# The first two column pairs of layer 2's feed-forward as eight plain products by token halves

## The chip, the cores and the metric

The kernel runs on one core of a Trainium2 chip. The metric is device time in microseconds (us) of one execution. Before the change the median of three runs is 1791.24 us (1790.11 to 1793.18). The profiled execution took 1794.53 us, of which its span is 1792.7 us.

## The reference

Two layers of a backbone over 512 latent tokens and 256 context tokens, width 1024, feed-forward width 2816, all in float32. The change is in the feed-forward of layer 2, which only the latent tokens pass:

```python
def _swiglu(h, w_in, w_out):
    g, u = jnp.split(h @ w_in, 2, axis=-1)
    return (jax.nn.silu(g) * u) @ w_out
...
    x = x + g2 * _swiglu(_rmsnorm(x, norm_w[layer, 1]) * (1.0 + sc2) + sh2, ffn_w_in[layer], ffn_w_out[layer])
```

## The kernel before

**Tiling.** Activations are held feature-major: 8 blocks of 128 features by 512 latent tokens. A float32 product is made of three passes in the format fp32r: an operand is split into a high and a low part (`h`, `lo`), and high·high, high·low and low·high are summed in PSUM. ScalarE (ACT) casts the high part, VectorE (DVE) subtracts it to get the low one. So one product over 4 feature blocks and 256 tokens is 12 matmuls of 128x256.

**Seven products instead of eight.** For each of the 22 blocks of 128 columns of the input projection (a *pair*: the block `g` and its partner `u`) the two matrices, split into upper and lower feature rows (r = 0, 1), and the tokens, split into the halves LA and LB, form a 2x2 by 2x2 block product. It is computed with seven products of 12 matmuls instead of eight. They need sums on the activation side (the *forms* `t2`, `t3`, `n1`, `n4` beside the plain `b11`, `b21` of LA and `b12`, `b22` of LB) and sums on the weight side (`z`, `y`, made per pair on DVE in tiles `ws`). Of the seven, only the two with `b11` and `b21` can start with LA alone; the forms of the other five need LB.

**What comes before.** The output projection of attention (`pf`, from `oh`, `ol`) runs first over LA, then over LB. After each half DVE adds it to the stream `xt`, ACT squares it, GpSimd (POOL) adds the squares into `nacc`; TensorE (PE) sums over partitions (`nsum`), DVE adds epsilon (`v`), POOL takes the power -1/2 (`rs`), PE broadcasts it (`nbc`), and `norm_seven` makes the normed and modulated rows (tile `bb`: one DVE and one ACT instruction per feature block) and the forms (tile `hT`). With LA ready, `op_ffn_seven` computes `c11` (products `b11`, `b21`, bank `pg`) of pairs 0 and 1, then waits for LB; `rest` computes the other five products of a pair in banks `pu`. After every four pairs the output projection of four pairs (`outproj`, bank `pf`, from the activations `fu`) follows.

**Order of the work.** The program is recorded by generators ("streams") that a small planner (`Flow.run`) interleaves by estimated times; what is recorded is then in a fixed order on each engine. Each engine takes its instructions strictly in that order, so an instruction that waits holds up all behind it on the same engine. Weights come through `Weights.ask` on SP's DMA queue into three buffers `wr` of 512 KB; a buffer is asked for again when the instructions that split it have been recorded, and the DMA starts when they have run. `Weights.seven` splits a pair: `xh`, `xl` for `g` and for the lower half of `u`, `wh`, `wl` for the sums `z` and `y`.

In the trace nearly all instructions have one line, that of the helper which records them (L107), so tiles tell them apart.

Of the kernel before, what the change touches and what calls it, by code (L numbers as in the profile page):

```python
# [8 lines left out]
F32 = mybir.dt.float32  # L9
# [134 lines left out]
def kernel(ctx, tc, x, c, cx, c_ctx, ada_w, ada_b, norm_w, ffn_w_in, ffn_w_out, ab_w_in,  # L144
# [45 lines left out]
    def t3(name, dt=F32, n=512, bufs=None):  # L190
        return tmp.tile([P, n], dt, tag=name, name=nm(name), bufs=bufs)
# [289 lines left out]
    class Weights:  # L481
# [8 lines left out]
        def plan(self, specs):  # L490

            for sp in specs:
                i = len(self.todo)
                if sp[0] == "seven":
                    self.todo += sp[1:]
                    self.jobs.append((i, i + 1))
                else:
                    self.todo.append(sp)
                    self.jobs.append((i,))
# [34 lines left out]
        def seven(self, i, job):  # L534


            yield lambda: self.asked > job[1] and "pool" in F1
            yield spend((self.n_x, 1))
            flow.cur.t = max(self.at[j] for j in job)
            yield  # L540
            g, u = (self.raw.pop(j) for j in job)
            parts = {}

            def split(name, tiles, src):
                h, lo = tiles
                act.copy(h, src)
                dve.tensor_tensor(lo, src, f(h), ALU.subtract)
                parts[name] = h, lo

            def whl():  # L550
                return tuple(wp.tile([P, KT, P], F32R, tag=t, name=nm(t), bufs=3) for t in ("wh", "wl"))

            def sums():
                return F1["pool"].tile([P, KT, P], F32, tag="ws", name=nm("ws"), bufs=3)

            x = [F1["pool"].tile([P, 12, P], F32R, tag=t, name=nm(t), bufs=2) for t in ("xh", "xl")]
            split("g", [t[:, 0:8] for t in x], g)
            self.units[i] = parts
            yield
            z = sums()  # L560
            y = sums()
            dve.tensor_tensor(y[:, 0:4], g[:, 0:4], u[:, 0:4], ALU.add)
            dve.tensor_tensor(y[:, 4:8], u[:, 0:4], u[:, 4:8], ALU.add)
            yield
            dve.tensor_tensor(z[:, 0:4], y[:, 4:8], g[:, 0:4], ALU.add)
# [1267 lines left out]

    FORMS = ("b11", "b21", "t2", "t3", "n1", "n4", "b22")
    hT, b_ = [], {}

    def form(lo, name, q):

        i = 14 * lo + 2 * FORMS.index(name) + q
        while len(hT) <= i // 3:
            hT.append(big([P, 3, 2, 256], F32R, "hT"))
        return hT[i // 3][:, i % 3]

    def norm_seven(part):
# [8 lines left out]
        def rows(r, q):  # L1855

            name = ("b11", "b21") if first else ("b12", "b22")
            t = b_.get(name[r])
            if t is None:
                if first:  # L1860
                    t = F1["pool"].tile([P, 4, 256], F32, tag="bb", name=nm("bb"), bufs=2)
                else:
                    t = big([P, 6, 256], F32, "bb")
                b_[name[r]] = t
            for k in (2 * q, 2 * q + 1):
                kk = 4 * r + k
                dve.scalar_tensor_tensor(t[:, k], xk(xt, kk, a, b), amod[1][:, 1, kk, 0:1], bcs[:, 0:256],
                                         ALU.mult, ALU.mult)
                act.activation(t[:, k], t[:, k], AF.Identity, bias=mod[1][:, 24 + kk, 0:1])
            return t[:, 2 * q:2 * q + 2]  # L1870

        def two(name, q, src):
            h, lo = form(0, name, q), form(1, name, q)
            act.copy(h, src)
            return lambda: dve.tensor_tensor(lo, src, f(h), ALU.subtract)

        if first:
# [7 lines left out]
            late()  # L1885
            ready["g1done"].add(a)
            return
        late = []
        pair = lambda: t3("hfull").rearrange("p (k n) -> p k n", k=2)
        n1, t2 = [], []  # L1890
        sums = big([P, 3, 2, 256], F32, "bb")
        for q in range(2):
            b12, b22 = rows(0, q), rows(1, q)
            n1.append(sums[:, q])
            t2.append(sums[:, 2] if q else b_["b12"][:, 4:6])
            dve.tensor_tensor(n1[q], b_["b11"][:, 2 * q:2 * q + 2], b12, ALU.subtract)
            dve.tensor_tensor(t2[q], b22, n1[q], ALU.add)
            two("t2", q, t2[q])()
        for q in range(2):
            b12, b22 = (b_[n][:, 2 * q:2 * q + 2] for n in ("b12", "b22"))  # L1900
            t = pair()
            dve.tensor_tensor(t, b12, b22, ALU.subtract)
            two("t3", q, t)()
        for q in range(2):
            two("n1", q, n1[q])()
        for q in range(2):
            t = pair()
            dve.tensor_tensor(t, b_["b21"][:, 2 * q:2 * q + 2], t2[q], ALU.subtract)
            two("n4", q, t)()
        for q in range(2):  # L1910
            two("b22", q, b_["b22"][:, 2 * q:2 * q + 2])()
        ready["g1done"].add(a)

    def norm_then(part):
        def run():
# [7 lines left out]
    def op_ffn_seven(last):  # L1923
# [30 lines left out]
        def rest(fi, c11_later):  # L1954
            u, bank_a, m1 = there[fi][:3]
            pu = psum2("pu")
            bank_b, bank_d = pu[:, 0:256], pu[:, 512:768]
            yield lambda: "z" in u and LB[0] in ready["g1done"]
# [40 lines left out]
        def place(fi):  # L1999
# [6 lines left out]
                res.append(pieces.pop(0))  # L2006
            acts[fi] = res

        def inproj(fi):
            def gen():  # L2010
                place(fi)
                if fi == 0:
                    yield from c11(0)
                    c11_end(0)
                    flow.cur.t = 0.0
                    yield
                    yield from c11(1)
                    c11_end(1)
                    flow.cur.t = 0.0
                    yield  # L2020
                elif fi > 1:
                    yield from c11(fi)
                    flow.cur.t = 0.0
                    yield
                yield from rest(fi, fi > 1)
            c0 = P * fi
            op(gen, [("seven",) + tuple(wfeat(ffn_w_in[1, :, c:c + P]) for c in (c0, DFF + c0))])

        def outproj(fs):
            nk = len(fs)  # L2030
# [29 lines left out]
            else:  # L2060
                op(lambda: gen((LAT,)), specs)

        for fi in range(NF):
            inproj(fi)
            if fi % 4 == 1 and 4 < fi < NF - 4:
                outproj(list(range(fi - 5, fi - 1)))
        outproj(list(range(NF - 6, NF)))

    def store(k, part):
# [90 lines left out]
```

## Time and profile before

| | |
|---|---|
| median of the runs | 1791.24 us |
| profiled execution | 1794.53 us, span 1792.7 us |
| PE busy | 1728.4 us, 96% of the span, 11898 instructions |
| DVE busy | 1153.3 us, 64% |
| ACT busy | 688.7 us, 38% |
| POOL busy | 270.3 us, 15% |
| granted TensorE clock, mean | 0.978 of full speed |

The stretch that the change touches runs from about 1380 us of the span (end of attention's output projection) to about 1480 us (the first pairs); layer 2's feed-forward then goes on to the end. The page's second part shows the span in 40 slices of 45 us each; this stretch is shorter than one slice, so it is read from views of a few microseconds, below.

### The profile page before, as it was taken

The page shows a single profiled execution, that of the slowest core. Times are in us where ns is not written, and L with a number is a line of the kernel's source. Part 1 is how long each engine was busy: PE and PEld are TensorE (multiplying, and loading weights), DVE is VectorE, ACT ScalarE, POOL GpSimd, SP SyncE. Part 2 cuts the span into 40 slices and gives each one's busy share as a digit, 9 for nine tenths or more (in the row PEclk, how much of TensorE's full clock was granted, in tenths as well). Part 3 has the DMA queues.
Part 4 walks back from the last instruction along what each step waited for, and adds up shares of the span by engine and source line. Part 5 has one row for each costly group of instructions (what it writes and reads, how often), then busy time and mean ns, then how long its engine had stood idle before and what let it go on. Part 6 is the DMA issues. An engine that isn't in the chain of part 4 may idle for free.

```text
span 1792.7 us, 29501 instructions
## 1 busy us (share of the span) xinstructions
PE 1728.4 (96%) x11898; PEld 1532.6 (85%) x11898; DVE 1153.3 (64%) x2084; ACT 688.7 (38%) x1348; POOL 270.3 (15%) x265
## 2 busy tenths in 40 slices
PE   7899999999999999999999999898999899999998
PEld 5789899999878888888888888897667788999998
DVE  5855365756597376564544335778886887787785
ACT  4522334433425221212121124545775554443443
POOL 4202120211123000000000003335554300000000
PEclk8999899999999999999999999898999889999999
DMA  9511111111573254353542215221003523233335
GB/s 343 193 51 48 28 45 38 34 36 54 194 241 113 81 177 141 118 165 117 157 147 62 60 52 159 73 71 48 2 1 100 149 58 113 89 117 96 102 87 153
DMA packets 224557, 184.36 MB, mean 103 GB/s; under 512 B 7532, under 2 KB 206628, under 8 KB 224420
## 3 DMA queue, kind: packets, MB, share of 16 engines
q1 hardware_dynamic: 222468, 178.20, 32.6%
q10 hardware_dynamic: 1952, 4.27, 0.7%
q8 instruction: 94, 1.54, 0.4%
q14 instruction: 43, 0.35, 0.1%
HBM read 175.10 MB, written 7.34 MB: 102 GB/s over the span
## 4 chain that ended last, share of the span: by engine, by line
PE 82%; DVE 8%; DMA 3%; ACT 3%; issue 2%; POOL 1%; SPq 0%; DVEq 0%; POOLq 0%; ACTq 0%
PE pf L107 27%; PE pu L107 17%; PE pg L107 13%; PE pt L107 10%; PE sc L107 3%; PE ao L107 2%; DMA wr<-in_ffn_w_in_dram 2%; PE mo L107 2%; PE atr L107 2%; DVE wl L107 1%; PE ro L107 1%; DVE acc L107 1%; PE kv L107 1%; PE me L107 1%; PE ada L107 1%
## 5 line engine op out<-in xcount | busy, mean ns | idle before, releaser
L107 ACT CAST wh<-wr 128x1024 fp32r<-128x1024 f32 (+1 forms) x184 | 186.0, 1011 | 341.3 <-PE pf L107 171.4
L107 DVE TENSOR_TENSOR wl<-wr,wh 128x1024 fp32r<-128x1024 f32 (+1 forms) x184 | 222.6, 1210 | 105.7 <-ACT wh L107 104.6
L107 DVE SCALAR_TENSOR_TENSOR xt<-pf,mod,xt 128x512 f32<-128x512 f32 (+1 forms) x160 | 97.9, 615 | 90.2 <-PE pf L107 89.6
L107 POOL TENSOR_TENSOR nacc<-nacc,sq 128x256 f32<-128x256 f32 (+1 forms) x42 | 54.9, 1308 | 631.7 <-ACT sq L107 628.5
L107 PE MATMUL pu<-hT,wh 128*128 128x256 f32 x704 | 129.0, 284 | 1.8 <-ACT hT L107 1.8
L107 DVE TENSOR_TENSOR hfull<-pu,sq 128x512 f32<-128x512 f32 (+1 forms) x44 | 24.5, 558 | 149.8 <-PE pu L107 149.5
L107 PE MATMUL pf<-fh,wh 128*128 128x256 f32 (+1 forms) x352 | 119.3, 340 | 0.8 <-ACT wh L107 0.8
L107 PE MATMUL pf<-fl,wh 128*128 128x256 f32 (+1 forms) x352 | 118.5, 337 | 0.0
L107 PE MATMUL pf<-fh,wl 128*128 128x256 f32 (+1 forms) x352 | 118.0, 338 | 0.5 <-DVE wl L107 0.5
L107 PE MATMUL pf<-fu,wh 128*128 128x512 f32 (+1 forms) x448 | 116.7, 349 | 1.4 <-ACT fu L107 0.4
L107 DVE SCALAR_TENSOR_TENSOR acc<-aw,cmod,acc 128x1024 f32<-128x1024 f32 x90 | 115.0, 1300 | 0.0
L107 PEld LDWEIGHTS pu<-hT,wh 128*128 128x128 f32 x704 | 108.9, 191 | 3.0 <-ACT hT L107 2.4
L107 PE MATMUL pu<-hT,wl 128*128 128x256 f32 x352 | 97.9, 283 | 0.1
L107 PEld LDWEIGHTS pf<-fu,wh 128*128 128x128 f32 x448 | 77.2, 188 | 12.8 <-ACT fu L107 0.6
L107 PE MATMUL pt<-wh,hh 128*128 128x256 f32 x288 | 84.2, 294 | 3.4 <-ACT hh L107 2.2
L107 PE MATMUL pt<-wl,hh 128*128 128x256 f32 x288 | 83.6, 292 | 0.3 <-DVE wl L107 0.3
L107 PE MATMUL pg<-g0h,wh 128*128 128x512 f32 (+1 forms) x220 | 82.1, 373 | 1.5 <-ACT sq L107 1.5
L107 POOL TENSOR_TENSOR aE<-aE,ast 128x512 f32<-128x512 f32 (+1 forms) x64 | 72.9, 1153 | 66.9 <-DVE ast L107 51.6
L107 PE MATMUL pg<-g0l,wh 128*128 128x512 f32 (+1 forms) x220 | 82.3, 374 | 0.0
L107 PE MATMUL pt<-wh,hl 128*128 128x256 f32 x288 | 82.2, 288 | 0.0
L107 PE MATMUL pu<-g0l,wh 128*128 128x512 f32 (+1 forms) x220 | 82.0, 373 | 0.0
L107 PE MATMUL pu<-g0h,wh 128*128 128x512 f32 (+1 forms) x220 | 81.9, 372 | 0.0
(379 smaller groups left out, 5166.1 us busy)
## 6 DMA issues: line engine op xcount, KB each, us to landing
wr<-in_ffn_w_in_dram SPq DMA_DIRECT2D x88, 512.0 KB, 3.9
aw<-in_ada_w_dram SPq DMA_DIRECT2D x84, 512.0 KB, 5.0
wr<-in_ab_w_in_dram SPq DMA_DIRECT2D x32, 512.0 KB, 4.3
wr<-in_ffn_w_out_dram SPq DMA_DIRECT2D x32, 512.0 KB, 5.2
wr<-in_ffn_w_out_dram SPq DMA_DIRECT2D x32, 384.0 KB, 3.6
wr<-in_ab_w_out_dram SPq DMA_DIRECT2D x16, 512.0 KB
wr<-in_attn_w_out_dram SPq DMA_DIRECT2D x16, 512.0 KB, 4.2
aw<-in_ada_w_dram SPq DMA_DIRECT2D x8, 768.0 KB
```

What stands on the lines that cost most here:

```text
L107: r = fn(*a, **k)
```

## The change

Pairs 0 and 1 are computed with plain products, LA first: for each token half four products per pair (`g` and `u`, upper and lower rows), accumulated in one bank `pg` of 512 columns (left half `g`, right half `u`), then silu, product and split by halves of 256 tokens. Their weights are split as they are (`g` in `xh`, `xl`; all of `u` in `wh`, `wl`), without the sums `z` and `y`. LB's plain rows `b12`, `b22` are made and split first, then the forms, in place of the rows they come from, where before some had tiles of their own. The seven products start with pair 2. The output projection of four pairs follows after pairs 4, 8, 12 and 16 instead of 5, 9, 13 and 17.

```diff
@@ class Weights, seven()
+            if job[2] == "eight":
+                yield spend((self.n_p, 1))
+                split("u", whl(), u)
+                self.freed += 2
+                self.ask()
+                return
             z = sums()
...
-    FORMS = ("b11", "b21", "t2", "t3", "n1", "n4", "b22")
+    FORMS = ("b11", "b21", "b22", "t2", "t3", "n1", "n4", "b12")
...
@@ norm_seven(), part LB
+        for q in range(2):
+            for r in range(2):
+                two(("b12", "b22")[r], q, rows(r, q))()
+        ready["g1done"].add(a)
+        four = [[b_[n][:, 2 * q:2 * q + 2] for n in ("b11", "b21", "b12", "b22")] for q in range(2)]
+        t2 = [b_[n][:, 4:6] for n in ("b12", "b22")]
+        for q, (b11, b21, b12, b22) in enumerate(four):
+            dve.tensor_tensor(b11, b11, b12, ALU.subtract)
+            dve.tensor_tensor(t2[q], b22, b11, ALU.add)
+            two("t2", q, t2[q])()
+        for q, (b11, b21, b12, b22) in enumerate(four):
+            dve.tensor_tensor(b12, b12, b22, ALU.subtract)
+            two("t3", q, b12)()
+        for q, (b11, b21, b12, b22) in enumerate(four):
+            two("n1", q, b11)()
+        for q, (b11, b21, b12, b22) in enumerate(four):
+            dve.tensor_tensor(b21, b21, t2[q], ALU.subtract)
+            two("n4", q, b21)()
+        ready["g1done"].add("forms")
...
@@ op_ffn_seven()
+        PLAIN = 2
+        def plain():
+            us = {}
+            for part, names in ((LA, ("b11", "b21")), (LB, ("b12", "b22"))):
+                c = slice(part[0] - NCX, part[1] - NCX)
+                for fi in range(PLAIN):
+                    if part is LA:
+                        place(fi)
+                        us[fi], = yield from W.take(1)
+                        yield lambda: "u" in us[fi]
+                    yield lambda: part[0] in ready["g1done"]
+                    ps = wide_bank("pg")
+                    for i, t in enumerate("gu"):
+                        for r, name in enumerate(names):
+                            product(ps[:, 256 * i:256 * i + 256], us[fi][t], 4 * r, name, start=r == 0)
+                    if part is LB:
+                        W.give(1)
+                        W.n_x.n += 1
+                    th, tl = acts[fi]
+                    sg, cc = t3("sq")[:, 0:256], t3("hfull")[:, 0:256]
+                    act.activation(sg, ps[:, 0:256], AF.Silu)
+                    dve.tensor_tensor(cc, ps[:, 256:512], sg, ALU.mult)
+                    act.copy(th[:, c], cc)
+                    dve.tensor_tensor(tl[:, c], cc, f(th[:, c]), ALU.subtract)
+                    flow.cur.t = 0.0
+                    yield
...
-        for fi in range(NF):
+        op(plain, [("eight",) + columns(fi) for fi in range(PLAIN)])
+        for fi in range(PLAIN, NF):
             inproj(fi)
-            if fi % 4 == 1 and 4 < fi < NF - 4:
-                outproj(list(range(fi - 5, fi - 1)))
+            if fi % 4 == 0 and 0 < fi < NF - 4:
+                outproj(list(range(fi - 4, fi)))
         outproj(list(range(NF - 6, NF)))
```

On PE, at the end of attention's output projection, the order before was this (`pf` is that projection, `pg` the first product of pair 0; numbers belong to buffers):

```order
L107 MATMUL pf_2166_13929<-ol_2000_12969,wh_2158_13874 128x256
L107 MATMUL pf_2166_13929<-oh_1999_12968,wl_2159_13876 128x256
L107 MATMUL nsum_2172_13970<-cst_74,nacc_94 128x1 x2
L107 MATMUL pg_2174_13976<-hT_2134_13713,xh_2163_13909 128x256
L107 MATMUL pg_2174_13976<-hT_2138_13717,xh_2163_13909 128x256
L107 MATMUL pg_2174_13976<-hT_2134_13713,xl_2164_13910 128x256
```

After the change the same `nsum` and `nbc` stand here on PE (`pg_2171` is pair 0 over LA, `pg_2192` pair 1 over LA):

```order
L107 MATMUL pg_2171_13969<-hT_2135_13720,wh_2164_13939 128x256
L107 MATMUL nsum_2169_13963<-cst_74,nacc_94 128x1 x2
L107 MATMUL pg_2171_13969<-hT_2137_13728,wh_2164_13939 128x256
L107 MATMUL pg_2171_13969<-hT_2135_13720,wl_2165_13940 128x256
L107 MATMUL pg_2171_13969<-hT_2135_13720,wh_2164_13939 128x256
L107 MATMUL pg_2171_13969<-hT_2137_13728,wh_2164_13939 128x256
L107 MATMUL pg_2171_13969<-hT_2135_13720,wl_2165_13940 128x256
L107 MATMUL nbc_2176_14028<-cst_74,rs6_93 128x128 x2
L107 MATMUL pg_2192_14098<-hT_2134_13713,xh_2174_14024 128x256 x2
```

Before, `nsum` stood directly behind the last `pf`, with 12 matmuls between it and `nbc`. Now 43 of the 48 matmuls of pair 0 over LA stand ahead of `nsum`, and only five between it and `nbc`.

On DVE, the step `v` (written `v6`) between `nsum` and `nbc` stood before among sums of pair 1 and pair 2 (`ws`, from the loads `wr`), in this order:

```order
L107 TENSOR_TENSOR wl_2178_14006<-ws_2167_13942,wh_2177_14005 128x1024
L107 TENSOR_SCALAR v6_92<-nsum_2172_13970 128x2
L107 TENSOR_TENSOR wl_2192_14068<-ws_2168_13943,wh_2191_14067 128x1024
L107 TENSOR_TENSOR ws_2195_14075<-ws_2196_14076,wr_2160_13878 128x512
L107 TENSOR_TENSOR ws_2216_14218<-wr_2171_13968,wr_2200_14112 128x512
```

Now it stands here (`wr_2167` and `wr_2190` are the two loads of pair 2, `wr_2166` is `u` of pair 1, `hfull` the first activation product of pair 0):

```order
L107 TENSOR_TENSOR wl_2189_14091<-wr_2166_13943,wh_2188_14090 128x1024
L107 TENSOR_TENSOR ws_2207_14297<-wr_2167_13945,wr_2190_14094 128x512
L107 TENSOR_TENSOR ws_2207_14297<-wr_2190_14094 128x512
L107 TENSOR_TENSOR ws_2206_14296<-ws_2207_14297,wr_2167_13945 128x512
L107 TENSOR_SCALAR v6_92<-nsum_2169_13963 128x2
L107 TENSOR_TENSOR ws_2206_14296<-ws_2206_14296,wr_2167_13945 128x512
L107 TENSOR_TENSOR hfull_2173_14019<-pg_2171_13969,sq_2172_14018 128x256
L107 SCALAR_TENSOR_TENSOR bb_2177_14031<-xt_2084_13370,amod1_176,nbc_2176_14028 128x256 x2
```

Three sums of pair 2 now stand ahead of `v`, the first of which reads both loads of pair 2; before, the first sum over both loads of pair 2 stood behind `v`.

## Rows read from the trace of the kernel before

**Rows 1.** Page, part 4: shares of the chain that ended last, by engine.

```profile
PE 82%; DVE 8%; DMA 3%; ACT 3%; issue 2%; POOL 1%; SPq 0%; DVEq 0%; POOLq 0%; ACTq 0%
```

**Rows 2.** Busy time by stretch: us, each engine with instructions, clock, DMA share, GB/s.

```profile
1380.00:1400.00 20.00, 20.00 (x172) 20.00 (x171) 11.97 (x15) 9.24 (x15) 9.07 (x7) 1.00 0.65 187
...
1417.60:1421.50 3.90, 0.19 (x2) 0.00 (x0) 3.27 (x6) 1.12 (x4) 2.38 (x2) 1.00 0.47 134
1421.50:1445.30 23.80, 17.36 (x72) 15.89 (x73) 20.50 (x35) 13.92 (x26) 1.62 (x1) 0.50 0.23 67
...
1450.00:1750.00 300.00, 299.15 (x2149) 281.08 (x2150) 237.72 (x355) 124.80 (x181) 0.00 (x0) 1.00 0.34 100
```

**Rows 3.** PE in order of time: start, us, instruction [idle before <-releaser].

```profile
1421.52 1.01 PE L107 MATMUL nsum<-cst,nacc 128*128 128x1 f32 x4 [3.73 <-POOL nacc L107]
...
1426.30 1.22 PE L107 MATMUL nbc<-cst,rs 128*128 128x128 f32 x4 [1.00 <-POOL rs L107]
1427.18 0.77 PE L107 MATMUL pg<-hT,xh 128*128 128x256 f32 x2
...
1449.99 0.47 PE L107 MATMUL pu<-hT,xh 128*128 128x256 f32 x2 [0.61 <-DVE u L107]
```

**Rows 4.** PE's groups from 1417.6 to 1449.9, first and last of four.

```profile
L107 PE MATMUL pg<-hT,xh 128*128 128x256 f32 x32 | 10.7, 435 | 3.6 <-ACT sq L107 3.0 <-ACT m L107 0.6
...
L107 PE MATMUL pu<-hT,wl 128*128 128x256 f32 x16 | 5.0, 318 | 0.0
```

**Rows 5.** PE in order of time, at half and at full clock.

```profile
1427.96 0.63 PE L107 MATMUL pg<-hT,xh 128*128 128x256 f32 x2
...
1429.24 0.63 PE L107 MATMUL pg<-hT,xh 128*128 128x256 f32 x2
...
1460.20 0.28 PE L107 MATMUL pu<-hT,wl 128*128 128x256 f32 x1
...
1462.33 0.40 PE L107 MATMUL pu<-hT,wh 128*128 128x256 f32 x2
```

**Rows 6.** Page, part 6: DMA issues, with size and median us to landing.

```profile
wr<-in_ffn_w_in_dram SPq DMA_DIRECT2D x88, 512.0 KB, 3.9
```

**Rows 7.** ACT in order of time, the load of pair 1's g.

```profile
1416.79 1.05 ACT L107 CAST xh<-wr 128x1024 fp32r<-128x1024 f32 x1 [1.93 <-DMA wr<-in_ffn_w_in_dram]
```

**Rows 8.** DVE in order of time, from the first loads to pair 2's sums.

```profile
1413.30 0.47 DVE L107 SCALAR_TENSOR_TENSOR xt<-pf,mod,xt 128x256 f32<-128x256 f32 x1
...
1421.45 0.69 DVE L107 TENSOR_TENSOR ws<-wr,wr 128x512 f32<-128x512 f32 x1 [0.62 <-DMA wr<-in_ffn_w_in_dram]
...
1424.40 0.15 DVE L107 TENSOR_SCALAR v<-nsum 128x2 f32<-128x2 f32 x1
...
1427.92 0.69 DVE L107 TENSOR_TENSOR ws<-wr,wr 128x512 f32<-128x512 f32 x1 [1.64 <-DMA wr<-in_ffn_w_in_dram]
```

**Rows 9.** POOL in order of time, the power after each half's sum.

```profile
1398.64 0.71 POOL L107 TENSOR_TENSOR rs<-v,mhalf 128x2 f32<-128x2 f32 x1 [2.38 <-DVE v L107]
...
1424.63 1.62 POOL L107 TENSOR_TENSOR rs<-v,mhalf 128x2 f32<-128x2 f32 x1 [3.17 <-DVE v L107]
```

**Rows 10.** DVE in order of time, rows and forms of LB, and a later load.

```profile
1402.43 3.22 DVE L107 SCALAR_TENSOR_TENSOR bb<-xt,amod,nbc 128x256 f32<-128x256 f32 x8 [0.62 <-POOL nacc L107]
...
1432.87 1.22 DVE L107 TENSOR_TENSOR wl<-ws,wh 128x1024 fp32r<-128x1024 f32 x1
1434.00 0.69 DVE L107 TENSOR_TENSOR bb<-bb,bb 128x512 f32<-128x512 f32 x1
...
1447.20 0.76 DVE L107 TENSOR_TENSOR u<-pu,m 128x256 f32<-128x256 f32 x2
...
1470.28 0.69 DVE L107 TENSOR_TENSOR ws<-wr,wr 128x512 f32<-128x512 f32 x1 [2.74 <-DMA wr<-in_ffn_w_in_dram]
```

**Rows 11.** Busy time by stretch, around an idle time of PE in attention.

```profile
1230.20:1233.10 2.90, 0.13 (x3) 0.09 (x2) 2.90 (x6) 2.51 (x4) 0.00 (x0) 1.00 0.05 14
1233.80:1244.00 10.20, 8.77 (x40) 7.32 (x38) 9.03 (x23) 5.43 (x15) 4.80 (x3) 0.50 0.28 83
```

More of the change, by code (lines that the diff above doesn't have):

```diff
@@ L493, in plan @@
                 i = len(self.todo)
-                if sp[0] == "seven":
+                if sp[0] in ("seven", "eight"):
                     self.todo += sp[1:]
-                    self.jobs.append((i, i + 1))
+                    self.jobs.append((i, i + 1, sp[0]))
                 else:
@@ L538, in seven @@
             yield spend((self.n_x, 1))
-            flow.cur.t = max(self.at[j] for j in job)
+            flow.cur.t = max(self.at[j] for j in job[:2])
             yield
-            g, u = (self.raw.pop(j) for j in job)
+            g, u = (self.raw.pop(j) for j in job[:2])
             parts = {}
@@ L1832 @@
     LA, LB = (NCX, NCX + 256, 0), (NCX + 256, NT, 0)
-    FORMS = ("b11", "b21", "t2", "t3", "n1", "n4", "b22")
+    FORMS = ("b11", "b21", "b22", "t2", "t3", "n1", "n4", "b12")
     hT, b_ = [], {}
     def form(lo, name, q):
-        i = 14 * lo + 2 * FORMS.index(name) + q
+        i = 4 * FORMS.index(name) + 2 * lo + q
         while len(hT) <= i // 3:
@@ L1887, in norm_seven @@
             return
[L1888 to L1891, printed above, removed]
         for q in range(2):
[L1893 to L1897, printed above, removed]
-            two("t2", q, t2[q])()
[L1899 to L1912, printed above, removed]
+            for r in range(2):
[6 more added lines that the diff above has]
+            dve.tensor_tensor(t2[q], b22, b11, ALU.add)
+            two("t2", q, t2[q])()
+        for q, (b11, b21, b12, b22) in enumerate(four):
[7 more added lines that the diff above has]
+        ready["g1done"].add("forms")
     def norm_then(part):
@@ L1957, in rest @@
             bank_b, bank_d = pu[:, 0:256], pu[:, 512:768]
-            yield lambda: "z" in u and LB[0] in ready["g1done"]
+            yield lambda: "z" in u and "forms" in ready["g1done"]
             product(bank_b, u["z"], 0, "t2")
@@ L2007, in place, with columns @@
             acts[fi] = res
+        def columns(fi):
+            return tuple(wfeat(ffn_w_in[1, :, c:c + P]) for c in (P * fi, DFF + P * fi))
+        PLAIN = 2
[24 more added lines that the diff above has]
+                    yield
         def inproj(fi):
@@ L2011, in gen @@
                 place(fi)
-                if fi == 0:
-                    yield from c11(0)
-                    c11_end(0)
+                if fi == PLAIN:
+                    yield from c11(fi)
+                    c11_end(fi)
                     flow.cur.t = 0.0
                     yield
-                    yield from c11(1)
-                    c11_end(1)
+                    yield from c11(fi + 1)
+                    c11_end(fi + 1)
                     flow.cur.t = 0.0
                     yield
-                elif fi > 1:
+                elif fi > PLAIN + 1:
                     yield from c11(fi)
@@ L2024, in gen @@
                     yield
-                yield from rest(fi, fi > 1)
-            c0 = P * fi
-            op(gen, [("seven",) + tuple(wfeat(ffn_w_in[1, :, c:c + P]) for c in (c0, DFF + c0))])
+                yield from rest(fi, fi > PLAIN + 1)
+            op(gen, [("seven",) + columns(fi)])
         def outproj(fs):
```

## The prediction

> **What bounds the kernel now.** I read the chain that ended last first: PE holds 82% of it [rows 1], so a change pays where PE idles or runs slowly. Busy time by stretch shows where that is. From 1450 to 1750 us PE is busy 299.15 of 300 us at full clock; from 1417.60 to 1421.50 it does next to nothing, and from 1421.50 to 1445.30 it is busy 17.36 of 23.80 us at a granted clock of 0.50, the lower of its two levels, 1.2 GHz [rows 2]. PE in order of time names the waits: 3.73 us for POOL's sum of squares of LB (so PE had ended at 1417.79), then 1.00 for the power, and several more up to 1449.99, after which it runs through [rows 3]. That is the price of norming LB: with LA alone PE had only the 48 matmuls of `c11` of pairs 0 and 1 to do.
>
> The stretch from 1417.79 to 1449.99 is 32.2 us. It holds 96 matmuls of the feed-forward: four groups, the first of 32, the last of 16, and two of the same sizes between [rows 4]. At full clock 18 matmuls take 1462.33 - 1460.20 = 2.13 us, 0.118 each; at half clock six take 1429.24 - 1427.96 = 1.28 us, 0.213 each [rows 5]. So 96 x 0.118 = 11.3 us is work, and **20.9 us are lost** (with `nsum` and `nbc` counted as lost). The change can win at most that.
>
> **The change part by part.**
>
> *Work added.* Two pairs with eight products instead of seven: 2 x 12 = 24 matmuls x 0.118 = **2.8 us** on PE, which nothing hides, since PE runs through afterwards.
>
> *First wait.* 43 matmuls of pair 0 over LA (43 x 0.118 = 5.1 us) now stand ahead of `nsum`, which then comes at about 1417.7 + 5.1 = 1422.8. Before, the sum of squares was there at 1421.5 [rows 3], and nothing that makes it is later now. The 3.73 us go. `nsum` itself costs some 0.5 us at full clock (half of its 1.01 at half clock). The 48 matmuls are done at about 1423.9.
>
> *Second wait, at `nbc`.* This is what is late next. Between `nsum` and `nbc` PE has only five matmuls, and `v` stands on DVE behind three sums that need both loads of pair 2. Those loads wait for buffers. Pair 0's `g` is split directly after the DVE instruction at 1413.30 (0.39 to the next one, then a split of 1.13), so its buffer is free and `u` of pair 1 is issued at 1414.85; it lands 3.9 us later [rows 6], at 1418.75. Pair 2's two loads queue behind it. The stretch 1380 to 1400 moved 187 GB/s [rows 2], that is 2.8 us for a load of 512 KB, so they land at 1421.5 and 1424.35. The second can't land before 1422.9: its buffer held pair 1's `g`, whose cast began at 1416.79 [rows 7] and took 1.05, then 1.13 for the split and 3.9 for the load. If the three loads do not overlap at all it lands at 1414.85 + 3 x 3.9 = 1426.55. Three sums of 0.60 (0.69 less the 0.09 by which DVE's instructions overlap) put `v` at 1426.15. From `v` to the power it took 0.23 us [rows 8, 9], and from the power's start to `nbc` 1.67 [rows 9, 3], of which 1.62 is the power; after LA the same power took 0.71. So `nbc` starts between 1427.1 and 1428.05; I take the middle, 1427.6, since one DVE sum runs beside it for part of that time. PE waits 1427.6 - 1423.9 = **3.7 us** (bounds: 1425.7 and 1430.25, so 1.8 to 6.4).
>
> The Trainium skill has a reason for the two durations of the power: GpSimd's SBUF interface is shared with VectorE and is contended by DVE instructions with two SBUF inputs ("GPSIMD Engine Reference", section 1, Specifications). The sum behind `v` is such an instruction; by the rule alone the wait would be 4.2 us and the forecast 0.5 us later, and with no contention 3.2 us.
>
> *The clock after that wait.* Idle times of this size brought the clock down in this trace: after the 3.73 us it was 0.50 [rows 2], and in attention, after 2.8 us with next to no matmuls, it read 0.50 for the 10 us that followed [rows 11]. I take it that it falls here too and is back after pair 1's 48 matmuls over LA. Then `nbc` costs 0.88 (1426.30 to 1427.18, [rows 3]) and the 48 matmuls 48 x (0.213 - 0.118) = 4.6 us more: **5.4 us**. What they hide: on DVE the rows and forms of LB follow `nbc`. Up to the last plain form of `b12` these are eight rows x 0.40 (3.22 for eight), one split 1.13, eight sums or splits x 0.60 and two short ones x 0.34 [rows 10]: 9.8 us. It starts some 1.2 us after `nbc`, so that form is there at 1438.6; PE at half clock comes at 1427.6 + 0.9 + 10.2 = 1438.7 and doesn't wait. If the clock stays up, PE is through at 1433.7, has 14 more matmuls (1.7 us) that need the first half of `b12` alone, and waits from 1435.4 to 1438.2: 2.8 + 0.4 for `nbc` = 3.2 us. So the two ways differ by 2.2 us only, since DVE sets the pace of the one.
>
> The Trainium skill's page "TensorE: Matmul & The Clock Gate" (sections "What's actually happening" and "HAM oscillation") says that the low clock is the default, which activity releases and idle gaps bring back. It speaks against this change, which makes a new gap. By it 5.4 us is right, as the trace's two falls say; without a fall the sum would be 2.2 us better.
>
> *First pairs with seven products.* Pairs 0 and 1 no longer need `z` and `y`: per pair four sums x 0.60 go, two splits of 1.13 go while that of `u` grows from 0.60 to 1.13, and of the final combinations half goes. LB's extra plain form costs two splits x 0.60. DVE so gets several us less to do. But pair 3's sums and pair 4's stand in DVE's queue in front of each other's splits, and each waits for loads that start only when the forms are done. Such waits of DVE were 0.62, 1.64 and 2.74 us before [rows 8, 10]. Then PE was covered; here its lead has just been used up. I take their mean, **1.7 us**, with bounds 0 and 2.7.
>
> *Nothing.* The sums in place save buffers, and no instruction. The output product one pair sooner issues the same matmuls and loads in another order; the last of the four activations it reads is one pair old, and the PE work of a pair (84 x 0.118 = 9.9 us) hides its split. Without that cover each of four places would cost PE a DVE or ACT step of 0.6 us, up to 2.4 us in all; I take 0.
>
> **Sum.** 2.8 + 0.5 + 3.7 + 5.4 + 1.7 = 14.1 us in place of 20.9: 6.8 us less. The rows are of an execution of 1794.53 us (span 1792.7 and 1.8 around it), 3.3 above the median of the runs; I take the difference off the median: 1791.24 - 6.8 = **1784.4 us**.
>
> **Rivals.**
>
> *The clock stays up.* For it: PE runs at full clock without a break up to the wait, and the wait may be short. Against it: both falls in [rows 2, 11]. 2.8 + 0.5 + 3.7 + 3.2 + 1.7 = 11.9, a gain of 9.0: 1782.2 us. With the shortest wait (1.8) and no wait at pair 3 it is 8.3, a gain of 12.6: 1778.6.
>
> *The wait has only moved.* The loads of pair 2 come one after the other, `nbc` waits 6.4 us, and pair 3 waits its 2.7: 2.8 + 0.5 + 6.4 + 5.4 + 2.7 = 17.8, a gain of 3.1: 1788.1, no change that can be told. For it: DVE did wait for both of pair 2's loads before, until 1427.92 [rows 8]; against it: one buffer is free 2 us sooner now.
>
> *Slower: the clock stays low.* Before, half clock lasted 23.8 us, because wait after wait broke PE's run [rows 2, 3]. In the changed kernel PE takes LB's forms as they come. If short waits keep the clock down over pair 1's LA (48), LB of both pairs (96) and pair 2's first 24 matmuls, that is 168 x 0.095 = 16.0 in place of 4.6: 25.5 us, a loss of 4.6: 1795.8. It decides from 48 + 6.8 / 0.095 = 120 matmuls at half clock on. Against it: behind the half-clock run the forms are there, so there is little left to break it.
>
> **How the numbers follow.** Chances: forecast 0.60, clock up 0.20, wait moved 0.13, clock low 0.07. A measurement of this kernel tells 0.2% or 3.6 us from no change, so faster is below 1787.6 and slower above 1794.8. Faster: nearly all of the forecast (0.57), all of the second, a quarter of the third (0.03): 0.80. Slower: of the last 0.05. The rest, 0.15, is no change. The range leaves out the best end of the second case and most of the last: 1779.5 to 1790.0.
>
> **What would show it.** In the changed profile: no wait of PE at `nsum`; a wait at `nbc` of 2 to 6 us, with `v` on DVE behind three `ws`, the first ended by a DMA; the granted clock at 0.50 for about 10 us behind it; no wait over 1 us for LB's forms; then one or two waits on PE for a low part `wl` or `xl` within the next pairs; 1872 in place of 1848 matmuls that read `hT`. The forecast is wrong if `nsum` still waits, if PE waits at `nbc` for over 8 us, if half clock lasts for 20 us, or if waits of over 1 us at the `pf` products of the four output products appear.

## The result, and the profile after

| | before | after |
|---|---|---|
| median (9 runs each) | 1791.4 us (1786.7 to 1793.56) | 1780.36 us (1777.42 to 1785.55) |
| ratio | | 0.9943, 95% interval 0.9929 to 0.9957 |
| profiled execution | 1794.53 us, span 1792.7 | 1785.55 us, span 1783.7 (the longest of the nine) |
| end of attention's output projection to end of span | 374.9 us | 366.6 us |
| PE / DVE busy | 1728.4 / 1153.3 us | 1723.7 / 1142.7 us |

The changed kernel is 11.0 us faster by the medians, and the interval of the ratio is clear of 1. A gain of 6.8 us was forecast, and a time of 1784.4 us; the measured 1780.36 lies inside the forecast range. Of the nine executions the shortest (1777.42 to 1778.55) had a mean granted clock of 0.988 to 0.989 and the longest (1781.71 to 1785.55) one of 0.983 to 0.986, so a single profile, here the longest of the nine, shows where the clock fell in one execution only. The chain that ended last holds a little more PE than in [rows 1]; this is the page's line:

```profile
PE 84%; DVE 8%; ACT 3%; issue 3%; DMA 2%; POOL 1%; SPq 0%; POOLq 0%; ACTq 0%; DVEq 0%
```

Busy time by stretch, to be laid beside [rows 2] (us, engines with instructions, granted clock, DMA share, GB/s). The attention part ended 0.65 us earlier in this execution (1417.14 against 1417.79).

```profile
1417.60:1421.50 3.90, 3.90 (x36) 3.90 (x34) 2.44 (x3) 1.37 (x2) 2.80 (x2) 1.00 0.83 227
1421.50:1445.30 23.80, 18.35 (x137) 17.54 (x136) 19.29 (x37) 15.03 (x28) 1.14 (x1) 0.93 0.11 29
1427.80:1431.10 3.30, 3.30 (x15) 3.30 (x16) 2.04 (x4) 2.26 (x5) 0.00 (x0) 0.50 0.00 0
1431.20:1461.80 30.60, 27.73 (x227) 26.91 (x227) 27.36 (x48) 17.66 (x34) 0.00 (x0) 1.00 0.24 70
1461.90:1465.20 3.30, 3.24 (x16) 2.95 (x15) 2.61 (x5) 0.00 (x0) 0.00 (x0) 0.50 0.00 0
```

Where PE stood still before (0.19 of 3.90 us busy) it is now fully busy. The next 23.8 us were all at a granted clock of 0.50; now the clock is at 0.50 for two short stretches of some 3.4 us, one behind each of PE's two longer waits. PE in order of time shows these waits (start, us, instruction, idle before and what ended it), to be laid beside [rows 3]:

```profile
1422.09 0.50 PE L107 MATMUL nsum<-cst,nacc 128*128 128x1 f32 x4
...
1427.80 1.22 PE L107 MATMUL nbc<-cst,rs 128*128 128x128 f32 x4 [4.52 <-POOL rs L107]
1428.67 0.77 PE L107 MATMUL pg<-hT,xh 128*128 128x256 f32 x2
...
1437.82 0.50 PE L107 MATMUL pg<-hT,xh 128*128 128x256 f32 x2 [0.69 <-ACT hT L107]
...
1438.95 0.38 PE L107 MATMUL pg<-hT,xh 128*128 128x256 f32 x1 [0.23 <-DVE hT L107]
...
1460.89 0.38 PE L107 MATMUL pu<-hT,wl 128*128 128x256 f32 x1 [1.94 <-DVE wl L107]
```

`nsum` has no wait any more. `nbc` has one of 4.52 us, where 1.00 stood. DVE in order of time tells why, beside [rows 8]:

```profile
1424.43 0.69 DVE L107 TENSOR_TENSOR ws<-wr,wr 128x512 f32<-128x512 f32 x1 [3.83 <-DMA wr<-in_ffn_w_in_dram]
1425.04 0.68 DVE L107 TENSOR_TENSOR ws<-wr 128x512 f32<-128x512 f32 x1
1425.76 0.69 DVE L107 TENSOR_TENSOR ws<-ws,wr 128x512 f32<-128x512 f32 x1
1426.37 0.15 DVE L107 TENSOR_SCALAR v<-nsum 128x2 f32<-128x2 f32 x1
...
1458.40 0.69 DVE L107 TENSOR_TENSOR ws<-wr,wr 128x512 f32<-128x512 f32 x1 [2.38 <-DMA wr<-in_ffn_w_in_dram]
```

The tiny `v`, whose input `nsum` was there at 1422.5, stands behind three sums, and the first of these waits 3.83 us for pair 2's second load. POOL's power follows (1426.60, 1.14 us), then `nbc`. The last row is the same pattern later: DVE waits for a load of pair 4, and PE gets pair 3's low part `wl`, which stands behind that sum, 1.94 us late (the pairs by the order of sums and splits on DVE).

### The profile page after: what moved, and what is told of

Same layout as the page of the kernel before. It is cut to its first block, busy times and chain, and to the rows that moved or that the text cites. A ratio compares the mean times of both kernels' runs of the same rounds, so it can differ in the third digit from the quotient of the medians.

```text
span 1783.7 us, 29532 instructions
## 1 busy us (share of the span) xinstructions
PE 1723.7 (97%) x11922; PEld 1529.8 (86%) x11922; DVE 1142.7 (64%) x2068; ACT 685.4 (38%) x1346; POOL 270.7 (15%) x265
## 4 chain that ended last, share of the span: by engine, by line
PE 84%; DVE 8%; ACT 3%; issue 3%; DMA 2%; POOL 1%; SPq 0%; POOLq 0%; ACTq 0%; DVEq 0%
PE pf L107 28%; PE pu L107 18%; PE pg L107 14%; PE pt L107 10%; PE sc L107 3%; PE ao L107 2%; PE mo L107 2%; PE atr L107 2%; PE ro L107 1%; DVE wl L107 1%; DVE acc L107 1%; PE kv L107 1%; PE me L107 1%; PE ada L107 1%; DVE hfull L107 1%
## 5 line engine op out<-in xcount | busy, mean ns | idle before, releaser
L107 PE MATMUL pu<-hT,wh 128*128 128x256 f32 x640 | 115.5, 281 | 0.0
L107 PEld LDWEIGHTS pu<-hT,wh 128*128 128x128 f32 x640 | 97.9, 188 | 0.7 <-ACT hT L107 0.2
L107 PE MATMUL pu<-hT,wl 128*128 128x256 f32 x320 | 87.9, 281 | 1.9 <-DVE wl L107 1.9
```

The costliest lines, as they stand in the source:

```text
L107: r = fn(*a, **k)
```

## The experiments

One theory and three rivals to begin with. **A**, the forecast's: the real work over LA covers the norm of LB; the price is PE's 24 extra matmuls, the wait at `nbc` and the clock. Rivals: **B**, DVE's work decides (less of it for pairs 0 and 1); **C**, the output product one pair sooner; **D**, only the half clock of 23.8 us is what was saved. The recorded expectations use the letters loosely: that DVE's forms set the pace behind the norm goes by A for e3 and by B from e5 on.

All runs are set against the kernel before, timed beside them on the same chip (its medians: 1791.94 us for e1 to e4, 1791.73 for e5 to e8, 1792.73 for e9 to e12). "Tail" is the profiled execution's time from the last `pf` of attention's output projection to the end of the span; "half clock" is the time at 0.50 between 1415 and 1480 us. Both are of one execution.

| run | median us | ratio (95% interval) | tail us | half clock us |
|---|---|---|---|---|
| before | | | 374.9 | 23.9 |
| changed kernel | 1780.36 | 0.9943 (0.9929 to 0.9957) | 366.6 | 6.8 |
| e1_old_out | 1781.46 | 0.9939 (0.9923 to 0.9956) | 363.8 | 3.4 |
| e2_one_plain | 1781.29 | 0.9945 (0.9929 to 0.9961) | 365.0 | 10.2 |
| e3_cover_before | 1786.63 | 0.9973 (0.9961 to 0.9985) | 370.4 | 10.2 |
| e4_dve_work_back | 1788.05 | 0.9979 (0.9969 to 0.9989) | 371.4 | 13.7 |
| e5_power_first | 1779.14 | 0.9935 (0.9917 to 0.9952) | 364.2 | 6.8 |
| e6_rows_first | 1776.86 | 0.9923 (0.9907 to 0.9938) | 361.6 | 3.4 |
| e7_both | 1778.24 | 0.9929 (0.9914 to 0.9944) | 360.4 | 3.4 |
| e8_dead_sums | 1784.51 | 0.9967 (0.9956 to 0.9979) | 368.4 | 10.2 |
| e9_wait_filled | 1785.09 | 0.9953 (0.9940 to 0.9966) | 367.7 | 6.8 |
| e10_filled_rows_first | 1782.95 | 0.9946 (0.9934 to 0.9958) | 364.5 | 0 |
| e11_24_left_out | 1784.09 | 0.9949 (0.9934 to 0.9964) | 366.5 | 10.2 |
| e12_left_out_rows_first | 1778.82 | 0.9925 (0.9912 to 0.9938) | 361.5 | 3.4 |

**e1_old_out: the output product at its old place.**

```diff
-            if fi % 4 == 0 and 0 < fi < NF - 4:
-                outproj(list(range(fi - 4, fi)))
+            if fi % 4 == 1 and 4 < fi < NF - 4:
+                outproj(list(range(fi - 5, fi - 1)))
```

> The changed kernel, with the four output products back where they stood before (one pair later); all else as changed. Theory A (the feed-forward over LA and the eight plain products carry the whole gain): nothing changes against the changed kernel, ratio to the kernel before 0.994, within 0.002. Rival C (the output product one pair sooner is a part of the gain): the part that it carries is given back, so a ratio of 0.996 to 1.000, with waits of PE at the pf products behind 1480 us that the changed kernel doesn't have.

Ratio 0.9939, and no wait over 0.5 us at `pf` behind 1480 us in either kernel. C falls. The execution also shows the changed kernel's beginning without the second fall of the clock. Its waits at `nbc` and for `wl` are shorter, as PE's rows say:

```profile
1425.88 0.71 PE L107 MATMUL nbc<-cst,rs 128*128 128x128 f32 x4 [3.55 <-POOL rs L107]
1426.35 0.48 PE L107 MATMUL pg<-hT,xh 128*128 128x256 f32 x2
...
1458.04 0.38 PE L107 MATMUL pu<-hT,wl 128*128 128x256 f32 x1 [1.36 <-DVE wl L107]
```

**e2_one_plain: one plain pair** (`PLAIN = 1` for `PLAIN = 2`).

> The changed kernel with one plain pair instead of two. PE then still has 96 matmuls over LA (48 of the plain pair, 48 of the first products of the next two) and 12 fewer added ones. Theory A in its bare form (PE counts alone): the same cover and 12 x 0.118 = 1.4 us less work, so 1.4 us faster than the changed kernel, ratio 0.993. Rival B (the work that DVE no longer has to do for pairs 0 and 1 carries a part): DVE has four sums and the splits of one pair (about 4 us) more in front of LB's forms, so 2 to 4 us slower than the changed kernel, ratio 0.995 to 0.9965.

0.9945, not to be told from two plain pairs, and the interval holds A's number and a part of B's, so the run does not choose between them. PE's rows show the wait at another place: `nbc` is hardly waited for, LB's first form for 6.50 us. Two things meet there. 48 of the 96 matmuls over LA now stand behind pair 0's products over LB, so nothing covers the wait; and DVE, busy with the sums of later pairs, starts LB's rows 5.1 us after the start of `nbc` (at 1425.87), where the changed kernel took 1.3.

```profile
1425.87 0.87 DVE L107 SCALAR_TENSOR_TENSOR bb<-xt,amod,nbc 128x256 f32<-128x256 f32 x2
```

```profile
1420.78 0.71 PE L107 MATMUL nbc<-cst,rs 128*128 128x128 f32 x4 [0.24 <-POOL rs L107]
...
1427.99 0.58 PE L107 MATMUL pg<-hT,xh 128*128 128x256 f32 x1 [6.50 <-ACT hT L107]
```

**e3_cover_before: the kernel before, with work for nothing in its wait.**

```diff
-            product(bank_a, u["g"], 0, "b11", stop=False)
+            for _ in range(4 if fi == 0 else 1):
+                F1["fill"] = product(bank_a, u["g"], 0, "b11", stop=False)
...
@@ norm_seven(), the matmuls of nsum
+            if not first:
+                order(z, F1["fill"])
```

> The kernel before, with the first product of pair 0 over LA (12 matmuls on b11) made four times into the same bank and LB's sum of squares behind them on PE: 48 matmuls at 0.118 = 5.7 us stand where PE waited 3.73 us. They are work for nothing, put there to keep the clock up. PE then reaches the sum of squares about 1423.4 instead of 1421.5, with 12 of its 96 matmuls done. Theory A (LB's forms on DVE set the pace behind the norm): the granted clock stays at 1.00, but PE's waits for the forms grow by as much, time within 2 us of the kernel before, ratio 0.999 to 1.0015. Rival D (what the change saved is the 23.8 us at half clock): at least 84 x 0.095 = 8.0 us come back, less the 2 us of fill, so about 6 us faster, ratio 0.9965 or less.

About 5 us faster (0.9973), between the two and nearer to D. So 36 matmuls that compute nothing new give nearly half of what the change gives, and the premise of this expectation, that DVE's forms alone set the pace behind the norm, does not hold in the kernel before. The clock, by stretch: it stays up through the norm and falls only later, for 10.2 us in place of 23.9, over PE's waits for forms.

```profile
1415.00:1426.00 11.00, 7.43 (x58) 6.75 (x57) 9.19 (x18) 6.90 (x11) 1.42 (x2) 1.00 0.44 123
1426.20:1436.30 10.10, 6.28 (x28) 5.69 (x27) 10.10 (x18) 6.56 (x14) 0.00 (x0) 0.50 0.06 17
```

**e4_dve_work_back and e8_dead_sums: the changed kernel with dead work on DVE.** In e4 each split of pairs 0 and 1 is made three times; in e8 the sums and two more instructions stand behind the split of `u`, in tiles that nobody reads.

```diff
 e4
-                dve.tensor_tensor(lo, src, f(h), ALU.subtract)
+                for _ in range(3 if job[2] == "eight" else 1):
+                    dve.tensor_tensor(lo, src, f(h), ALU.subtract)
 e8
                 split("u", whl(), u)
+                z = sums()
+                y = sums()
+                dve.tensor_tensor(y[:, 0:4], g[:, 0:4], u[:, 0:4], ALU.add)
...
+                dve.tensor_tensor(y, z, y, ALU.subtract)
+                dve.tensor_tensor(z, z, y, ALU.subtract)
```

> The changed kernel with dead work on DVE: each of the two splits on DVE of pairs 0 and 1 is made three times into the same tile, 8 more instructions of 1.13 us, 9.0 us, about what the change took off DVE there (four sums, two splits and part of a third for each pair, some 4.1 us x 2). Theory A in its bare form (PE's cover alone): DVE waited for loads for 3.8 us there and PE has cover for some of the rest, so 0 to 3 us slower than the changed kernel, ratio 0.994 to 0.9955. Rival B (the relief of DVE carries most of the gain): 6 to 9 us slower than the changed kernel, ratio 0.9975 to 0.9995.

> The changed kernel with dead work on DVE behind the split of u for pairs 0 and 1: the four sums of 0.60 us and two instructions of 1.13 us on whole tiles that the seven products would need, into tiles that nobody reads (2 x 4.7 = 9.3 us on DVE). PE's products wait for none of them. Theory A in its bare form (PE's cover alone; DVE waited 3.8 us for loads at this place): 0 to 3 us slower than the changed kernel, ratio 0.994 to 0.9955. Rival B (the relief of DVE carries a large part): 4 to 8 us slower than the changed kernel, ratio 0.996 to 0.9985, with longer waits of PE at LB's forms and a longer stretch at half clock.

e4 is 6.4 us slower than the changed kernel (0.0036 of 1791, the intervals apart), but not for one reason: PE waits for the repeated split itself, which it needs at once. This is PE's wait by cause in e4 (total, times, longest):

```profile
PE pg L107 <- DVE xl L107: 4.3, 1, 4.3
PE pg L107 <- DVE bb L107: 1.6, 1, 1.6
```

e8 has no such fault, and is 4.3 us slower (0.0024 of 1791). The two intervals just touch (0.9956 and 0.9957); taken as independent, they put the difference at 0.0024 ± 0.0018, so 1 to 7.5 us. B holds for that much. Its waits by cause:

```profile
PE nbc L107 <- POOL rs L107: 3.1, 1, 3.1
PE pu L107 <- ACT wh L107: 2.6, 1, 2.6
PE pg L107 <- DVE bb L107: 1.3, 1, 1.3
PE pg L107 <- ACT hT L107: 0.8, 1, 0.8
```

The wait at `nbc` does not grow (DVE only waited for loads there); the dead work comes out behind it, at LB's rows and at pair 2's sums. Two reservations: by DVE's busy time e8 brings back 7.5 us (1150.2 against 1142.7) of the 10.6 that the change took off; and its dead sums read the loads `wr`, so these buffers come free later and the next loads start later, as they did in the kernel before. In the changed kernel no load moved any more from 1427.80 to 1431.10; in e8, from 1429.10 to 1432.40, DMA ran at 187 GB/s:

```profile
1429.10:1432.40 3.30, 3.30 (x18) 3.30 (x17) 2.40 (x6) 0.29 (x1) 0.00 (x0) 0.50 0.63 187
```

So the 4.3 us are the price of DVE's work and of the later loads together.

**e5_power_first, e6_rows_first, e7_both: which limit is next.**

```diff
 e5: pair 2's sums behind v
-            dve.tensor_tensor(y[:, 0:4], g[:, 0:4], u[:, 0:4], ALU.add)
-            dve.tensor_tensor(y[:, 4:8], u[:, 0:4], u[:, 4:8], ALU.add)
+            order(dve.tensor_tensor(y[:, 0:4], g[:, 0:4], u[:, 0:4], ALU.add), F1["v"])
+            order(dve.tensor_tensor(y[:, 4:8], u[:, 0:4], u[:, 4:8], ALU.add), F1["v"])
 e6: LB's rows in the order in which PE reads them
-        for q in range(2):
-            for r in range(2):
+        for r in range(2):
+            for q in range(2):
                 two(("b12", "b22")[r], q, rows(r, q))()
 e7: both, and the sums over LB's forms behind the last of these
-            dve.tensor_tensor(b11, b11, b12, ALU.subtract)
+            order(dve.tensor_tensor(b11, b11, b12, ALU.subtract), last)
```

> The changed kernel with the three sums of pair 2, which wait for loads, ordered on DVE behind the short instruction v that feeds the power of LB's norm. Theory A (the new wait at nbc is what is left to win): the wait at nbc falls from 3.5 to 4.5 us to 1 us or less and the granted clock stays up behind it, 3 us of waiting and up to 1.7 us of half clock: 3 to 4.5 us faster than the changed kernel, ratio to the kernel before 0.992. Rival B (behind the norm DVE's rows and forms of LB set the pace, and pair 2's sums now stand between them): the wait only moves to PE's products on LB's forms, 0 to 1 us faster, ratio 0.9935 to 0.994.

> The changed kernel with LB's plain forms made in the order in which PE reads them: both halves of b12, then both of b22, where the change makes the first halves of both first. The same instructions. Theory A (PE runs behind DVE there, only 0.9 us of waits for forms): at most 0.9 us faster than the changed kernel, ratio 0.9935 to 0.994. Rival B (DVE sets the pace): b12's second half comes two rows, a sum and a split (some 2.5 us) sooner, and 1.5 to 2.5 us are won, ratio 0.9925 to 0.993.

> The changed kernel with v ahead of pair 2's sums, LB's plain forms in the order in which PE reads them, and the sums over LB's forms ordered behind the last plain form. If the wait at nbc and DVE's forms behind it are two limits of which the later one decides (B), only both edits together pay: 3.5 to 5 us faster than the changed kernel, ratio 0.9915, and more than the sum of the two edits alone. If A holds, it is what the first edit alone gives, within 1 us.

e5: 0.9935, 1.4 us faster by the ratios, not to be told from the changed kernel. The wait at `nbc` is gone (0.35 us) and stands at LB's forms instead, as B said:

```profile
1420.49 0.71 PE L107 MATMUL nbc<-cst,rs 128*128 128x128 f32 x4 [0.35 <-POOL rs L107]
...
1429.14 0.47 PE L107 MATMUL pg<-hT,xh 128*128 128x256 f32 x2 [1.53 <-DVE bb L107]
...
1434.13 0.58 PE L107 MATMUL pg<-hT,xh 128*128 128x256 f32 x1 [1.57 <-DVE hT L107]
```

e6: 0.9923, 3.6 us faster than the changed kernel by the ratios, more than its 0.9 us of waits for forms could give. PE's only wait over 0.35 us between 1410 and 1480 is that at `nbc`; the clock is low behind it alone, and the wait one pair later is gone:

```profile
1427.30 0.71 PE L107 MATMUL nbc<-cst,rs 128*128 128x128 f32 x4 [3.69 <-POOL rs L107]
```

```profile
1427.95:1431.30 3.35, 3.35 (x18) 3.35 (x17) 3.25 (x7) 2.83 (x7) 0.00 (x0) 0.50 0.00 0
1431.40:1770.00 338.60, 336.82 (x2471) 317.90 (x2470) 266.18 (x402) 145.68 (x224) 0.00 (x0) 1.00 0.36 106
```

e7: 0.9929, no more than e6, and the 0.9915 that B named is at the very edge of its interval (0.9914 to 0.9944), though its tail is the shortest of all runs and none of PE's waits from 1405 to 1480 us is over 1.04 us. That one is for a `wh` at 1451.48; 0.56 us for `u` follow at 1452.54, and the clock fell behind them:

```profile
1451.48 0.50 PE L107 MATMUL pu<-hT,wh 128*128 128x256 f32 x2 [1.04 <-ACT wh L107]
...
1452.54 0.61 PE L107 MATMUL pu<-hT,xh 128*128 128x256 f32 x2 [0.56 <-DVE u L107]
```

```profile
1452.85:1456.15 3.30, 3.30 (x17) 3.30 (x16) 3.30 (x5) 1.04 (x2) 0.00 (x0) 0.50 0.13 45
```

e6 and e7 are versions that beat both kernels by their medians; against the changed kernel the intervals overlap (0.9907 to 0.9938 and 0.9929 to 0.9957 for e6), so its lead of 3.6 us is likely and not shown.

**e9_wait_filled and e10_filled_rows_first: the wait at `nbc` filled with work for nothing.**

```diff
                         for r, name in enumerate(names):
-                            product(ps[:, 256 * i:256 * i + 256], us[fi][t], 4 * r, name, start=r == 0)
+                            for n in range(4 if (part is LA, fi, i, r) == (True, 0, 1, 0) else 1):
...
+                                z = product(ps[:, 256 * i:256 * i + 256], us[fi][t], 4 * r, name, start=r == 0,
+                                            behind=F1[hold] if hold else None)
@@ rms_bc(), the matmuls of nbc
+            if behind:
+                order(z, F1[behind])
```

The first line makes the product four times; `hold` is `nsum` for the three added ones, and `nbc` is ordered behind the last of them.

> The changed kernel with the wait at nbc filled: after LB's sum of squares PE makes the product of pair 0's u over b11 three more times into the same bank, 36 matmuls or 4.2 us of work for nothing where it waited 3.5 to 4.5 us, and only then takes nbc. The granted clock stays up behind nbc. Theory A (PE's waits and its clock are the loss): the 3.41 us at half clock give back 1.7 us, at most 2 us faster than the changed kernel, ratio 0.993. Theory B (behind the norm DVE's rows and forms set the pace): what PE wins it waits for at LB's forms, 0 to 1 us slower than the changed kernel, ratio 0.994 to 0.995.

> The same 36 matmuls for nothing in the wait at nbc, in the kernel with LB's rows in PE's order (e6_rows_first). There the waits for LB's forms were 0.2 us in all. Theory A: 1.7 us faster than e6_rows_first, ratio 0.9915. Theory B: the forms come just as PE needs them at half clock, so at full clock PE waits 1 to 2 us for them and the time stays within 1 us of e6_rows_first, ratio 0.992 to 0.993.

Neither is faster than the kernel it is made from: e9 is not to be told from the changed kernel (0.0010, or 1.8 us, slower by the ratios; A's 0.993 is outside its interval), and e10 is 4.1 us slower than e6 (0.0023; the intervals overlap by 0.0004), although e10's clock does not fall from 1415 to 1760 us:

```profile
1415.00:1760.00 345.00, 341.23 (x2489) 320.77 (x2488) 267.68 (x409) 148.89 (x227) 4.66 (x4) 1.00 0.36 104
```

DVE's rows show a likely cause for e10 being slower than B said. The fill stands inside pair 0's product, so that pair's activation (`hfull`) came late on DVE, and LB's rows (`bb`) stand behind it:

```profile
1427.67 1.23 DVE L107 TENSOR_TENSOR wl<-ws,wh 128x1024 fp32r<-128x1024 f32 x1 [1.17 <-ACT wh L107]
1429.37 0.42 DVE L107 TENSOR_TENSOR hfull<-pg,sq 128x256 f32<-128x256 f32 x1 [0.47 <-ACT sq L107]
1429.71 1.65 DVE L107 SCALAR_TENSOR_TENSOR bb<-xt,amod,nbc 128x256 f32<-128x256 f32 x4
```

From the end of attention's output projection, LB's first row starts at 13.0 us here and at 10.6 in e6, though `nbc` starts only 0.7 later (10.5 and 9.8). In e9 that row starts at 12.9, and its clock fell later, for 6.8 us. So these two runs don't measure the clock alone: they show that this fill wins nothing, and leave open what a full clock without a delay on DVE would give.

**e11_24_left_out and e12_left_out_rows_first: the 24 matmuls.**

```diff
                         for r, name in enumerate(names):
+                            if name == "b22" and t == "u":
+                                continue
                             product(ps[:, 256 * i:256 * i + 256], us[fi][t], 4 * r, name, start=r == 0)
```

> The changed kernel without 24 matmuls: the products of u with b22 for the first two pairs are left out, so that a part of the activations of these pairs is missing. It measures the term for the added work. The forecast's own step (nothing hides it, PE runs through behind): 24 x 0.118 = 2.8 us faster than the changed kernel, ratio 0.9925. Theory B (PE comes to its next wait that much sooner, at pair 2's and pair 3's sums and splits on DVE): 0 to 1.5 us faster, ratio 0.9935 to 0.994.

> The same 24 matmuls left out of the kernel with LB's rows in PE's order (e6_rows_first), with the same part of the activations missing. If PE is the bound there, 2.8 us faster than e6_rows_first, ratio 0.991; if DVE's sums and splits of pairs 2 to 4 are next in line, 0 to 1.5 us, ratio 0.9915 to 0.9925.

Both kernels leave out a part of the activations of pairs 0 and 1. Ratios 0.9949 and 0.9925, beside 0.9943 and 0.9923 with the 24 matmuls: no gain can be told in either. The 2.8 us that the forecast's step would give lie outside both intervals (0.9925 and 0.991); B's low end, nothing, is what came. In e11 PE comes sooner to its next wait, at a later pair's `u`, a step of DVE that stands behind sums of which the first waited 3.90 us for a load; the clock is at 0.50 around and behind it. PE's row, DVE's row, and the stretch:

```profile
1459.25 0.79 PE L107 MATMUL pu<-hT,xh 128*128 128x256 f32 x2 [3.00 <-DVE u L107]
```

```profile
1457.56 0.69 DVE L107 TENSOR_TENSOR ws<-wr,wr 128x512 f32<-128x512 f32 x1 [3.90 <-DMA wr<-in_ffn_w_in_dram]
```

```profile
1457.90:1464.60 6.70, 5.35 (x25) 5.36 (x26) 6.31 (x10) 1.57 (x2) 0.00 (x0) 0.50 0.01 2
```

## Why the prediction was right, and where its sizes failed

The sign, the place of the new wait and its cause were right; the gain was mis-sized by 4.2 us (6.8 for 11.0). By the steps:

- *No wait at `nsum`.* Right: gone in every run of the changed order. `nsum` itself took 0.36 us (1422.09 to 1422.45) for the 0.5 said.
- *Second wait, at `nbc`: 3.7 us.* Right in place, cause and size: 4.52 in the profiled execution, 3.55 in e1, 3.57 in e11, 3.69 in e6, each time with `v` behind three `ws` of which the first waits for a DMA. The power took 1.14 us, near the 1.17 for which the forecast's middle, 1427.6, stands. Counted from the end of `pf`, DVE's sum over both loads started 0.7 us later than worked out in the profiled execution, and 0.1 to 0.2 sooner in e1, e6 and e11.
- *The clock after that wait: 5.4 us.* **This term failed.** The step was that the clock "is back after pair 1's 48 matmuls", some 10 us, taken from [rows 2] and [rows 11]. It fell, but for 3.4 us: it read 0.50 from 1427.8 to 1431.1 and 1.00 from 1431.2 on, with PE busy all of the first. In the forecast's own terms that is 0.87 us for `nbc` (1427.80 to 1428.67), 1.1 for the matmuls of the next 2.5 us (12 x 0.095) and 0.92 for the waits at LB's forms (0.69 and 0.23): the term measures 2.9. The rows taken as model were stretches in which PE had further waits: in [rows 2] it is busy 17.36 of 23.80 us. The runs bear that difference out. Of the stretches at half clock in this part of the fourteen profiles, eight last 3.4 us, and PE runs through them; nine last 6.8 to 23.9 us, and PE waits 0.6 us or more within each.
- *Waits at pair 3: 1.7 us.* Right in kind: a low part `wl`, late because DVE waits for a load. That the size came out (1.94 us, and here some 1.5 more for a second fall of the clock) is in part chance, for it was the mean of three other waits: e1 has 1.36 and no fall, e6 0.31, and e11 3.00 with a fall.
- *Work added: 2.8 us that nothing hides.* The matmuls are there (1872 that read `hT`), but without them no gain can be told (e11, e12). PE doesn't run through behind them: in e11 it comes sooner to the next instruction that DVE, itself waiting for a load, holds up. In the sum the term is part of PE's time all the same.
- *Nothing.* Right for the output product (e1). For what DVE no longer does the text said "several us less to do" and gave no number. The sum needs none, since it counts only what PE loses in the changed kernel; but the forecast so could not say how much of the gain hangs on it, and e8 measures 4.3 us for giving most of it back.

With e1's sizes, whose profiled execution took 1781.76 us and so lies near the median, the forecast's own sum is 2.8 + 0.4 + 3.5 + 2.7 (0.47 for `nbc`, 16 x 0.095 = 1.5, and 0.71 at a form) + 1.4 = 10.8, and 20.9 - 10.8 = 10.1 us. 11.0 were measured, and the tails of before and e1 differ by 11.1 (374.9 - 363.8). So the clock's term, 2.7 where 5.4 stood, explains 2.7 of the 4.2 us, the other terms 0.6, and the last 0.9 us stay open.

Where the 11 us come from, by runs: filling the wait with dead matmuls gives some 5 (e3); real work over LA in its place, with most of DVE's work and its hold on the load buffers kept, some 6 (e8); taking that off 4.3 more; the output product nothing. The parts overlap, and how the 5 of e3 split between waits and clock is not settled, since its stretch at half clock went from 23.9 to 10.2 us while its waits moved too.

Of the rivals, "the clock stays up" (1782.2) named the smaller clock loss but not its reason, since the clock did fall; "the wait has only moved" had the right place with too high a price; "slower" did not come: the forms were there within 0.7 us of when PE was ready for them, and the clock was up again by then. By the Trainium skill ("TensorE: Matmul & The Clock Gate", "HAM oscillation") an idle gap brings the low clock back; the traces agree on the fall behind 3.5 to 4.5 us of waiting, and it does not follow that the low clock stays.

## What to carry to other kernels

A wait that is filled can come back at the next engine's limit: look there what the waiting engine will ask for next, in which order it is made, and which tiny instruction (here `v`) stands behind large ones that wait for loads. What a fall of the clock costs is read from a place where the engine ran unbroken behind its wait; a stretch with more waits in it shows the price of those too. And price the relief of an engine beside the one that bounds the kernel, and of the buffers that it holds: on a path where the two take turns, it can be worth as much as the wait that the change is about.

## What the runs showed of the hardware

- The clock fell behind short waits as well: behind 1.04 and 0.56 us in e7, and in e9 behind waits of 1.2 us at the longest; behind 1.4 us in e1 it did not. The length of one wait alone does not decide it in these traces.
- The power on POOL took 0.71 us with DVE idle (e5, e7), 1.14 beside one sum of 0.60 us, and 1.62 beside a split of 1.13 [rows 9]. POOL's row of the changed kernel, and that of e5:

```profile
1426.60 1.14 POOL L107 TENSOR_TENSOR rs<-v,mhalf 128x2 f32<-128x2 f32 x1 [5.41 <-DVE v L107]
```

```profile
1419.73 0.71 POOL L107 TENSOR_TENSOR rs<-v,mhalf 128x2 f32<-128x2 f32 x1 [1.65 <-DVE v L107]
```

  The Trainium skill ("SBUF — State Buffer", "Who interferes with whom") says that a DVE instruction with two SBUF inputs contends with a GpSimd instruction that reads SBUF, and that contention for the port pair they share is an exclusive lock. The trace agrees: the sum behind `v` ran from 1426.48 for 0.61 us, to 1427.09; 0.71 from there ends at 1427.80, and the power ended at 1427.74. The forecast's ends were 0.71 and the split's 1.62; its middle is near what the shorter sum gives.
- Busy shares alone don't tell here which engine is worth relieving. The Trainium skill ("Perfetto Trace Analysis", "Identifying the Most-Contended Engine") would optimise the engine with the highest occupancy first; for TensorE it judges by the share of weight loads and by the share of the peak reached. From 1410 to 1480 us of the changed kernel the weight loads are busy 61.16 of 70 us and DVE 55.27, so PE would come first; yet 24 matmuls fewer on PE brought no gain that can be told, and 7.5 us more of DVE's busy time cost 4.3. No run takes work off DVE alone.
